# A 448-byte tile ahead of the split weights' buffers in a one-layer transformer kernel

## The chip, the cores and the metric

The kernel runs on one core of one Trainium2 chip. The metric is the time of one execution on the device, in microseconds (us), as the median of several runs; lower is better.

## The reference

One layer over 512 tokens of width 1024, all in float32. What matters here are its matrix products:

```python
xn = rms_norm(h, norm_mix_g)
proj = xn @ w_in                                   # 1024 -> 4008 columns, cut into nine parts
# branch A: 8 heads of causal attention with forget gates; branch B: 8 latent heads with rotary keys
merged = gate_a * (ya @ w_branch_a) + gate_b * (yb @ w_branch_b)
h = h + merged @ w_out                             # 1024 -> 1024
hn = rms_norm(h, norm_ffn_g)
h = h + (silu(hn @ w_gate) * (hn @ w_up)) @ w_down # 1024 -> 2816 -> 1024
y = rms_norm(h, norm_final_g)
```

## The kernel before

Every product is made three times: each float32 operand is split into a part rounded to float32r (`hi`) and the rest (`lo`), and `mm3` (L124) adds hi x hi, hi x lo and lo x hi into one PSUM bank. `split` (L98) makes the parts: ScalarE writes `hi`, VectorE subtracts and writes `lo`. A matrix multiply on the tensor engine has two operands in SBUF: a stationary one of 128 columns, which a weight load (LDWEIGHTS, engine PEld in the profile) brings in, and a moving one of up to 512 columns (MATMUL, engine PE). The profile names a matmul as out<-moving,stationary.

The work goes in stages: the narrow columns of `w_in`; attention, with the remaining projections run between its steps (gates `pg<-x..`, queries and keys `pqa`, values `pva`, latent heads `pqb`, `pkb`, `pvb`, branch outputs `pb`); the output projection `po`; SwiGLU's gate and up strips (`pg<-h..`, `pu`, L932); and the down projection `pd` (L953), whose second column half cuts the last token tile into two parts of 256 columns (L958).

Weights come in pieces of 512 KB. `weights` (L130) takes a raw buffer (tag `wr`), loads it and calls `split_weights`, which takes three rotating buffers each for the parts:

```python
hi = big.tile([P, a, b], F32R, name="whi", tag="pt" if spare else "wh", bufs=4 if spare else 3)
lo = big.tile([P, a, b], F32R, name="wlo", tag="pt" if spare else "wl", bufs=4 if spare else 3)
```

All other large operands lie in the 17 buffers of 8192 bytes of the tag `u8`: `xTh`/`xTl`, `hTh`/`hTl`, `yah`.., `act`, `mgh`/`mgl`, `cq`, `kvs`, and for the output projection alone also the split weights `woh`/`wol` (L892).

The buffers of one partition lie one behind the other in the order in which their tags are first asked for, each rounded up to 32 bytes. From the tag `pt` on they are: 4 x 6656 bytes of `pt`, 1024 of `c1`, 17 x 8192 of `u8`, 2048 of `krs`, 4 x 2048 of `p`, then `rcol` and `post` with 16 bytes each, then 3 x 4096 of `wh` and 3 x 4096 of `wl`. The sizes up to `p` are multiples of 512, so `pt`, `u8`, `krs` and `p` begin at one place modulo 512 bytes; `rcol` and `post` take 32 bytes each, so `wh` and `wl` begin 64 bytes further on. Slices of operands that go into full matmuls begin at multiples of 512 bytes within their buffers. So a pair of operands is at equal places modulo 512 when both are in `pt` or `u8`, and 64 bytes apart when one is in `wh` or `wl`. In the first strip of the up projection, the pieces for the second half of the 1024 inputs go into `pt` (`spare`, L923, L937).

In the code below, the three parts of a product are made in `mm3`, and the loops that call it set the order of the stationary and moving operands.

Of the kernel before, what the change touches and what calls it, by code (L numbers as in the profile page):

```python
# [41 lines left out]
# columns of `cst`  # L42
# [4 lines left out]
def _turn_constants():  # L47
    """1/(2 pi) for angles cut into digits of 2^21, 2^11 and 2: each digit's share of a turn,
    without whole turns, as a part of 13 bits and the rest."""
    out = []  # L50
    for unit in (2.0 ** 21, 2.0 ** 11, 2.0):
        f = _frac_turn(unit)
        a = round(f * 8192.0) / 8192.0
        out.append((unit, a, f - a))
    return out


def _frac_turn(unit):
    from fractions import Fraction
    # pi to 50 digits  # L60
    pi = Fraction(314159265358979323846264338327950288419716939937510, 10 ** 50)
    t = Fraction(int(unit)) / (2 * pi)
    return float(t - round(t))
# [3 lines left out]
def tile_hybrid_fox_mla_block(  # L67
# [30 lines left out]
    def split(hi, lo, src, scale=None):  # L98
        """hi: src rounded to float32r; lo: what is left of it."""
        if scale is None:  # L100
            one = nc.scalar.copy(out=hi, in_=src)  # L101
            two = nc.vector.tensor_tensor(out=lo, in0=src, in1=hi.bitcast(F32), op=ALU.subtract)  # L102
        else:
            one = nc.scalar.activation(out=hi, in_=src, func=AF.Copy, scale=scale)  # L104
            two = nc.vector.scalar_tensor_tensor(out=lo, in0=src, scalar=scale, in1=hi.bitcast(F32),
                                                 op0=ALU.mult, op1=ALU.subtract)
        if pin[1]:
            tc.keep_in_program_order(one)
            tc.keep_in_program_order(two)

    # the tensor engine's work, and the parting of operands, in the order of the program
# [12 lines left out]
    def mm3(o, a, b, start, stop):  # L124
        """o += a^T b for a and b as (hi, lo)."""
        matmul(o, lhsT=a[0], rhs=b[0], start=start, stop=False)
        matmul(o, lhsT=a[0], rhs=b[1], start=False, stop=False)
        matmul(o, lhsT=a[1], rhs=b[0], start=False, stop=stop)

    def weights(src, a, b, spare=False):  # L130
        """A piece [128, a, b] of a weight (a * b <= 1024) as (hi, lo)."""
        raw = big.tile([P, a, b], F32, name="wraw", tag="wr", bufs=2)
        nc.sync.dma_start(out=raw, in_=src)
        return split_weights(raw, spare)
# [8 lines left out]
    def rsqrt(m, n, name, out=None):  # L143
        """v ** -0.5 for m = -4 v [128, n]: q = exp(-ln(4 v) / 2), then the Newton step q (3 - 4 v q^2)."""
        q = small([P, n], name + "_q")
        nc.scalar.activation(out=q, in_=m, func=AF.Ln, scale=-1.0)
        nc.scalar.activation(out=q, in_=q, func=AF.Exp, scale=-0.5)
        t = small([P, n], name + "_t")
        if n == 1:
            nc.vector.scalar_tensor_tensor(out=t, in0=q, scalar=m, in1=q, op0=ALU.mult, op1=ALU.mult)  # L150
        else:
            nc.vector.tensor_tensor(out=t, in0=m, in1=q, op=ALU.mult)
            nc.vector.tensor_tensor(out=t, in0=t, in1=q, op=ALU.mult)
        r = small([P, n], name + "_r") if out is None else out
        nc.vector.scalar_tensor_tensor(out=r, in0=t, scalar=3.0, in1=q, op0=ALU.add, op1=ALU.mult)
        return r

    def mean4(out, ss, width):
        """-4 times the guarded mean of a sum of squares."""
        nc.vector.tensor_scalar(out=out, in0=ss, scalar1=-4.0 / width, scalar2=-4.0 * EPS, op0=ALU.mult, op1=ALU.add)  # L160

    def mean_rsqrt(parts, width, name, out=None):
        """rsqrt of the mean of squares, from sums of squares [128, 1] in the order they come."""
        m = small([P, 1], name + "_m")
        mean4(m, parts[0], width)
        for p_ in parts[1:]:
            nc.vector.scalar_tensor_tensor(out=m, in0=p_, scalar=-4.0 / width, in1=m, op0=ALU.mult, op1=ALU.add)
        return rsqrt(m, 1, name, out)
# [22 lines left out]
    # before it takes its outputs: rotated q of the latent heads by token tile, the q rows of the chunk mask  # L191
# [4 lines left out]
    # rotary keys and the k rows of the chunk mask; from row 104 on: c in three parts  # L196
# [11 lines left out]
    def load_misc(c):  # L208
        if c == 0:
            # the first products wait for it: in two  # L210
            nc.sync.dma_start(out=mraw[0][:, 1, :], in_=w_in[P:2 * P, MISC0:GATE0])
            return
        raw = big.tile([P, 2, MISCW], F32, name="wraw", tag="wr" if c < 2 else "pt", bufs=2 if c < 2 else 4)
        nc.sync.dma_start(out=raw, in_=w_in[c * 256:(c + 1) * 256, MISC0:GATE0].rearrange("(k p) n -> p k n", p=P))
        mraw.append(raw)
# [19 lines left out]
    # products of zeros bring the tensor engine to its full clock  # L235
# [23 lines left out]
    def to_features(rows, hi, lo, t, tag):  # L259
        """Rows [128, 1024] of token tile t into hi/lo pairs [128, 4, 512]."""  # L260
        for c in range(2):
            pt = bank(tag, "ptr")
            for j in range(4):
                transpose128(pt[:, j * P:(j + 1) * P], rows[:, (4 * c + j) * P:(4 * c + j + 1) * P], ident)
            cols = slice(t * P, (t + 1) * P)
            split(hi[c][:, :, cols], lo[c][:, :, cols], pt.rearrange("p (j n) -> p j n", j=4))
# [4 lines left out]
    def rotary_angles():  # L271
        """cos and sin of positions * inv_freq, step by step."""
# [23 lines left out]
        # sin and cos of half the angle by their series, then of the angle itself  # L296
# [22 lines left out]
    rcol = small([P, NT], "rcol", bufs=1)  # L319
    pin[1] = True  # L320
    for st in "f0 k0 f1 t0 k1 f2 t1 f3 t2 m1 t3 f4 t4 m2 t5 f5 f6 t6 f7 m3 t7 w0 w1".split():
# [11 lines left out]
        else:  # L333
            # squares of x, added up over the tiles of features
# [12 lines left out]
    # 1 / rms by token: down the partitions, and along the columns  # L347
# [50 lines left out]
    def project_va(n):  # L398
        """Values of forgetting heads 4n to 4n + 3."""
# [19 lines left out]
    def gates(m):  # L419
        """Gate columns of tile m: 0..7 of the forgetting branch, 8..15 of the latent one."""  # L420
# [10 lines left out]
        # 1 / (1 + e) = exp(-ln(1 + e)); the bound keeps ln in its range  # L431
# [4 lines left out]
    def narrow(t0, n):  # L436
        """Of the narrow columns of n token tiles: norms of q and kv, forget gates, rotary key."""
# [38 lines left out]
    def step():  # L476
        """The gates' share between two steps of the latent heads' preparation."""
        for _ in range(next(stages, 0)):
            next(pre, None)
# [67 lines left out]
    def rotated_to_features():  # L547
        """Rotated q, scaled, as rows in two parts: four heads to a bank."""
# [14 lines left out]
    def project_b(j):  # L563
        """q and k of latent heads 2j and 2j + 1."""
# [26 lines left out]
    def project_a(j):  # L591
        """q and k of forgetting heads 2j and 2j + 1."""
# [23 lines left out]
        if j == 3:  # L616
            # the place of rbc is for outputs from here on
            moved = big.tile([P, S], F32, name="rbc", tag="krs", bufs=1)
            nc.gpsimd.tensor_copy(out=moved, in_=rbc[0])
            rbc[0] = moved  # L620

    def block(p_, i):
        """Of the packed P^T (keys kc, query q at column 384 kc + q), query block i of keys 0..i."""
        a = p_[:, i * P:(i + 1) * P]
        return bass.AP(a.tensor, a.offset, [a.ap[0], [PTS, i + 1], [1, P]])
# [4 lines left out]
    class Item:  # L630
        """Query block i of head h of branch b."""
# [62 lines left out]
    def branch(b, m2, done):  # L694
        """Tiles 2 m2 and 2 m2 + 1 of a branch's projection."""
# [47 lines left out]
    def running_sum():  # L743
        """c, the running sum of the logs of the forget gates, as rows in three parts."""
# [19 lines left out]
        # the first and the last cover all of the columns  # L764
# [15 lines left out]
    class Filler:  # L780
        """Projections to run between the steps of the attention, in order; weights in us of PE."""
# [62 lines left out]
    for n, it in enumerate(items):  # L844
        goal = rest + per * (len(items) - n - 1)
        if n and items[n - 1].i == NT - 1 and items[n - 1].h == NH - 1:
            # the branch's projection may follow at once
# [84 lines left out]
    for s in range(NHC // 2):  # L932
        # the first tiles take the first half of the tokens ahead of the rest
# [18 lines left out]
    ssf = small([P, 2 * NT + 1], "ssf", bufs=1)  # L952
    for half in range(2):  # L953
        nn = slice(half * 512, (half + 1) * 512)
        # parts of the columns, each with a bank: the last tile of the tokens in two
# [94 lines left out]
```

## Time and profile before

| what | value |
|---|---|
| time, median of 3 runs | 756.17 us (756.05 to 757.05) |
| span of the profiled execution, from first to last instruction | 754.7 us |
| PE busy | 739.7 us, 98% of the span |
| weight loads busy | 608.4 us, 81% |
| VectorE, ScalarE busy | 423.2 us, 336.1 us |
| HBM read | 66.59 MB, 91 GB/s over the span |

Of the profiled execution the profile gives the span alone; the median of the runs is 1.5 us above it. A matmul's busy time runs from its start to the modelled end of its pipeline, and two neighbours overlap; how fast matmuls follow each other is read from the distance of their starts in the timeline, not from the length of one.

### The profile page before, as it was taken

The numbers are of one execution on the slowest core, as the hardware profiler recorded it, in microseconds if no ns is written. First come the engines' busy times: TensorE is split into PE (matmuls) and PEld (weight loads), VectorE is DVE, ScalarE is ACT, GpSimd is POOL, SyncE is SP. The second block draws the span as 40 slices with busy tenths as digits, with TensorE's granted clock in tenths as the row PEclk, the third lists the DMA queues.
The fourth block names the chain that finished last, engine by engine and source line by source line (L and its number), as shares of the span: only waits on it lengthen the run. The fifth ranks groups of instructions, "written<-read, shape, count | busy, mean of one in ns | idle before, by whom it ended". The sixth has DMA issues, their size and how long they took to land.

```text
span 754.7 us, 9511 instructions
## 1 busy us (share of the span) xinstructions
PE 739.7 (98%) x3601; PEld 608.4 (81%) x3601; DVE 423.2 (56%) x818; ACT 336.1 (45%) x635; POOL 71.7 (10%) x87
## 2 busy tenths in 40 slices
PE   6999999999999999999999999999999999999996
PEld 4988677879888888887898888888888888888885
DVE  6998987666898986566733332233333233115224
ACT  7457977556675774534423223223232232113213
POOL 4243331011130120200000000000000000000000
PEclk9999999999999999999999999999999999999998
DMA  8522212031232221365303233232333322322312
GB/s 278 169 56 57 57 32 57 30 84 30 85 80 62 69 73 58 109 224 166 90 25 112 83 104 92 85 111 83 89 108 84 99 97 84 112 84 93 103 57 111
DMA packets 68941, 69.45 MB, mean 92 GB/s; under 512 B 3808, under 2 KB 58352, under 8 KB 68896
## 3 DMA queue, kind: packets, MB, share of 16 engines
q1 hardware_dynamic: 66240, 64.91, 28.5%
q10 hardware_dynamic: 1824, 3.38, 1.3%
q0 software_dynamic: 832, 0.57, 0.3%
q8 instruction: 28, 0.46, 0.2%
q14 instruction: 17, 0.14, 0.1%
HBM read 66.59 MB, written 2.10 MB: 91 GB/s over the span
## 4 chain that ended last, share of the span: by engine, by line
PE 90%; DVE 4%; ACT 3%; DMA 2%; issue 1%; SPq 0%; ACTq 0%; DVEq 0%
PE pg L115 26%; PE pu L115 16%; PE pd L115 15%; PE pqa L115 6%; PE pb L115 6%; PE po L115 6%; PE sp L115 4%; PE pva L115 3%; PE py L115 3%; PE pt L120 2%; DMA wraw<-in_w_in_dram 1%; PE pqb L115 1%; DMA wraw<-in_w_kv_up_dram 0%; PE ptr L120 0%; ACT xTh L104 0%
## 5 line engine op out<-in xcount | busy, mean ns | idle before, releaser
L102 DVE TENSOR_TENSOR wlo<-wraw,whi 128x1024 fp32r<-128x1024 f32 x102 | 125.2, 1227 | 205.3 <-ACT whi L101 204.8
L101 ACT CAST whi<-wraw 128x1024 fp32r<-128x1024 f32 x102 | 106.9, 1049 | 217.9 <-PE pu L115 81.6
L115 PE MATMUL pd<-whi,act 128*128 128x512 f32 (+1 forms) x396 | 110.6, 366 | 0.0
L115 PEld LDWEIGHTS pd<-whi,act 128*128 128x128 f32 x396 | 71.2, 188 | 12.4
L115 PE MATMUL pd<-wlo,act 128*128 128x512 f32 (+1 forms) x198 | 72.4, 366 | 0.0
L115 PE MATMUL pg<-hTh,wlo 128*128 128x512 f32 (+1 forms) x192 | 72.4, 377 | 0.0
L115 PE MATMUL pu<-hTh,whi 128*128 128x512 f32 (+1 forms) x192 | 72.3, 377 | 0.0
L115 PE MATMUL pu<-hTl,whi 128*128 128x512 f32 (+1 forms) x192 | 72.3, 377 | 0.0
L115 PE MATMUL pu<-hTh,wlo 128*128 128x512 f32 (+1 forms) x192 | 72.3, 377 | 0.0
L115 PE MATMUL pg<-hTl,whi 128*128 128x512 f32 (+1 forms) x192 | 72.2, 376 | 0.0
L115 PE MATMUL pg<-hTh,whi 128*128 128x512 f32 (+1 forms) x192 | 72.1, 376 | 0.0
L115 PE MATMUL pg<-xTh,whi 128*128 128x512 f32 x128 | 52.9, 413 | 0.0
L115 PE MATMUL pg<-xTl,whi 128*128 128x512 f32 x128 | 50.6, 395 | 0.0
L115 PE MATMUL pg<-xTh,wlo 128*128 128x512 f32 x128 | 50.5, 395 | 0.0
L115 PEld LDWEIGHTS pd<-wlo,act 128*128 128x128 f32 x198 | 37.2, 188 | 6.7
L115 PEld LDWEIGHTS pg<-hTh,whi 128*128 128x128 f32 x192 | 36.2, 188 | 7.3
L115 PEld LDWEIGHTS pu<-hTh,whi 128*128 128x128 f32 x192 | 36.2, 188 | 7.3
L115 PEld LDWEIGHTS pu<-hTl,whi 128*128 128x128 f32 x192 | 36.2, 188 | 7.2
L115 PEld LDWEIGHTS pu<-hTh,wlo 128*128 128x128 f32 x192 | 36.2, 188 | 7.2
L115 PEld LDWEIGHTS pg<-hTh,wlo 128*128 128x128 f32 x192 | 36.1, 188 | 7.2
L115 PEld LDWEIGHTS pg<-hTl,whi 128*128 128x128 f32 x192 | 36.1, 188 | 7.2
L432 POOL TENSOR_SCALAR gate<-gate 128x512 f32<-128x512 f32 x16 | 28.2, 1760 | 118.4 <-ACT gate L430 118.2
(280 smaller groups left out, 1437.0 us busy)
## 6 DMA issues: line engine op xcount, KB each, us to landing
wraw<-in_w_in_dram SPq DMA_DIRECT2D x28, 512.0 KB, 3.9
wraw<-in_w_ffn_gate_dram SPq DMA_DIRECT2D x22, 512.0 KB, 3.7
wraw<-in_w_ffn_up_dram SPq DMA_DIRECT2D x22, 512.0 KB, 3.8
wraw<-in_w_ffn_down_dram SPq DMA_DIRECT2D x22, 512.0 KB, 3.7
wraw<-in_w_out_dram SPq DMA_DIRECT2D x8, 512.0 KB, 4.3
xf<-in_xT_dram SPq DMA_DIRECT2D x8, 256.0 KB, 5.3
wraw<-in_w_branch_b_dram SPq DMA_DIRECT2D x4, 512.0 KB, 3.5
wraw<-in_w_branch_a_dram SPq DMA_DIRECT2D x4, 512.0 KB, 3.4
```

The source lines that it names most:

```text
L101: one = nc.scalar.copy(out=hi, in_=src)
L102: two = nc.vector.tensor_tensor(out=lo, in0=src, in1=hi.bitcast(F32), op=ALU.subtract)
L115: ins = nc.tensor.matmul(*args, **kw)
L120: ins = nc.tensor.transpose(*args)
L432: nc.gpsimd.tensor_scalar(out=g, in0=g, scalar1=1e30, scalar2=None, op0=ALU.min)
```

## The change

A tile of 112 float32 values (448 bytes a partition) is taken from the pool right after `rcol`, ahead of the first request for `post`, `wh` and `wl`, and GpSimd writes zeros into its first two columns. Nothing reads it. With it the buffers of `wh` and `wl` begin 64 + 448 = 512 bytes past the common place, which is the same place modulo 512. Comments and docstrings are taken out as well; they make no instructions.

```diff
     rcol = small([P, NT], "rcol", bufs=1)
+
+    shift = small([P, 112], "shift", bufs=1)
+    nc.gpsimd.memset(shift[:, 0:2], 0.0)
     pin[1] = True
     for st in "f0 k0 f1 t0 k1 f2 t1 f3 t2 m1 t3 f4 t4 m2 t5 f5 f6 t6 f7 m3 t7 w0 w1".split():
```

## Rows read from the trace of the kernel before

**Rows 1.** The page: busy time by engine, and the chain's shares by engine.

```profile
PE 739.7 (98%) x3601; PEld 608.4 (81%) x3601; DVE 423.2 (56%) x818; ACT 336.1 (45%) x635; POOL 71.7 (10%) x87
...
PE 90%; DVE 4%; ACT 3%; DMA 2%; issue 1%; SPq 0%; ACTq 0%; DVEq 0%
```

**Rows 2.** Waits: who waited for whom, us in total, times, longest.

```profile
ACT whi L101 <- PE pu L115: 81.6, 19, 4.6
...
PE pm L115 <- DVE mlo L102: 5.5, 2, 3.4
```

**Rows 3.** Busy time of engines in stretches; PEclk is the granted clock.

```profile
331.00:378.00 47.00, 46.20 (x211) 37.74 (x210) 32.01 (x51) 20.03 (x37) 0.00 (x0) 1.00 0.49 159
...
402.00:627.00 225.00, 225.00 (x971) 181.48 (x970) 74.97 (x81) 61.61 (x80) 0.00 (x0) 1.00 0.32 96
```

**Rows 4.** Timeline of PE (start us, length us), output projection: sixty matmuls apart.

```profile
355.61 0.39 PE L115 MATMUL po<-woh,mgh 128*128 128x512 f32 x1
...
369.21 0.39 PE L115 MATMUL po<-woh,mgh 128*128 128x512 f32 x1
```

**Rows 5.** Timeline of PE, gate and up strips: 195 matmuls apart.

```profile
560.02 0.40 PE L115 MATMUL pg<-hTl,whi 128*128 128x512 f32 x1
...
605.52 0.39 PE L115 MATMUL pg<-hTl,whi 128*128 128x512 f32 x1
```

**Rows 6.** Timeline of PE, down projection, first column half: 108 matmuls apart.

```profile
640.27 0.39 PE L115 MATMUL pd<-wlo,act 128*128 128x512 f32 x1
...
664.99 0.39 PE L115 MATMUL pd<-wlo,act 128*128 128x512 f32 x1
```

**Rows 7.** Timeline of PE, first up strip: 24 matmuls between each two rows.

```profile
385.92 0.28 PE L115 MATMUL pu<-hTh,whi 128*128 128x256 f32 x1
...
388.74 0.28 PE L115 MATMUL pu<-hTh,whi 128*128 128x256 f32 x1
...
391.62 0.28 PE L115 MATMUL pg<-hTh,whi 128*128 128x256 f32 x1
```

**Rows 8.** Timeline of PE, last part of the down projection: 33 matmuls apart.

```profile
743.74 0.28 PE L115 MATMUL pd<-wlo,act 128*128 128x256 f32 x1
...
747.48 0.28 PE L115 MATMUL pd<-wlo,act 128*128 128x256 f32 x1
```

**Rows 9.** Chain that ended last: start us, us, piece, instructions in it.

```profile
63.24 9.11 PE pg L115 x39
...
88.78 1.39 PE pqb L115 x6
...
118.86 1.40 PE pqa L115 x6
...
186.51 2.12 PE pva L115 x18
...
296.99 12.60 PE pg L115 x54
309.59 22.40 PE pb L115 x96
```

**Rows 10.** Groups of instructions by shape: count, busy us, mean ns, idle before.

```profile
L115 PE MATMUL pd<-whi,act 128*128 128x512 f32 x308 | 98.2, 391 | 0.0
L115 PE MATMUL pg<-hTh,whi 128*128 128x512 f32 x160 | 63.3, 396 | 0.0
...
L115 PE MATMUL pva<-whi,xTh 128*128 128x256 f32 x64 | 18.8, 294 | 0.0
...
L115 PE MATMUL pd<-whi,act 128*128 128x256 f32 x88 | 17.8, 276 | 0.0
```

**Rows 11.** Groups on VectorE and GpSimd: count, busy us, mean ns, idle before.

```profile
L102 DVE TENSOR_TENSOR wlo<-wraw,whi 128x1024 fp32r<-128x1024 f32 x102 | 125.2, 1227 | 205.3 <-ACT whi L101 204.8
...
L102 DVE TENSOR_TENSOR wol<-wraw,woh 128x1024 fp32r<-128x1024 f32 x8 | 9.8, 1222 | 7.8 <-ACT woh L101 7.8
...
L612 POOL MEMSET ha<- 6x512 f32 x8 | 4.3, 538 | 0.0
```

## The prediction

> **What bounds the kernel now.** I read the page first, for which engine sets the end: PE is busy for 98% of the span and is 90% of the chain that ended last [rows 1]. The list of waits says the same from the other side: the longest total wait of a PE matmul for another engine is 5.5 us, at the start, while ScalarE waits 81.6 us for PE to give back the up strip's weight buffers [rows 2]. So behind the first 40 us the time is a sum over matmuls, and what counts is how far apart their starts are.
>
> That is not in the mean length of a matmul, so I went to the timeline next and took the step, the distance of starts divided by the matmuls between, for full matmuls (128x512) of the same type in stretches where nothing else bounds:
>
> - output projection: (369.21 - 355.61) / 60 = 226.7 ns [rows 4];
> - gate and up strips: (605.52 - 560.02) / 195 = 233.3 ns [rows 5];
> - down projection: (664.99 - 640.27) / 108 = 228.9 ns [rows 6].
>
> The granted clock is 1.00, the 2.4 GHz level, in the stages of the first two [rows 3], and none of the three runs shows a wait. What differs is where the operands lie. In `po` both are in `u8` buffers, at equal places modulo 512. In the strips the stationary operand is in `wh` or `wl`, 64 bytes further on than the moving one. In `pd` it is the other way round. PE loads the next weights while the present matmul streams (both are busy most of the span, [rows 1]), so the two reads run at the same time, and the step is 6.6 ns longer where the weights lie one way apart, 2.2 ns where the other. The change puts all of these into the case of `po`.
>
> Half-width matmuls (128x256) tell another story, and I did not leave them out. In the first up strip 24 of them with weights in `wh` take (388.74 - 385.92) / 24 = 117.5 ns each, and the 24 behind them, whose weights lie in `pt` at equal places, (391.62 - 388.74) / 24 = 120.0 ns [rows 7]. The last part of `pd`, 64 bytes apart, steps at (747.48 - 743.74) / 33 = 113.3 ns [rows 8]. Equal places are best at 512 columns and worst at 256.
>
> **The change part by part.**
>
> The memset: the nearest row is a GpSimd memset of 538 ns [rows 11]. GpSimd is busy for 10% of the span [rows 1], and behind the new instruction on its queue stand only the additions of squares, which wait for ScalarE anyway. I take nothing; without that cover it is 0.5 us. The tile is written once and read by nobody, so it adds no wait.
>
> The splits: their outputs move by 448 bytes. `wlo` took 1227 ns at the old place and `wol`, already at the new one, 1222 [rows 11]. Nothing.
>
> Gate and up strips, full width: 160 matmuls in each of six groups [rows 10], 960 in all, from 233.3 to 226.7 ns: 960 x 6.6 = 6.4 us less. The floor is 226.7, under which no full matmul steps in any of these rows; the other end is no gain.
>
> Gates, queries and keys, branch outputs (128x512, weights in `wh`): some 750 between 40 and 331 us, but in short runs. Here I had to choose. The latent heads' `pqb`, at equal places already, take 1.39 us for six in such a run, and `pqa`, 64 bytes apart, 1.40 us [rows 9]: a run of six gains 0.01 us only, as if the good step needed a run to settle. The timeline has some 50 runs of six, which give 0.5 us, and some 50 of three, to which I give nothing. Three long runs, 39, 54 and 96 matmuls at 9.11 / 39 = 233.6 and 22.40 / 96 = 233.3 ns [rows 9], are worth 6.6 ns each; the last two follow each other. Leaving out nine at each start for settling (an allowance: a run of six has hardly gained yet), 162 x 6.6 = 1.1 us. Together 1.6 us less; the ends are 0 and, if every one of the 750 gained, 5.0.
>
> `pva`, half width, 64 matmuls in each of three groups [rows 10]: from 2.12 / 18 = 117.8 ns [rows 9] to 120.0, so 192 x 2.2 = 0.4 us more. If they went to 113.3 instead it would be 0.9 less.
>
> The first gate and up strip, half width: 144 matmuls from 117.5 to 120.0 ns, 0.4 us more; the other 48 are in `pt` already. At 113.3: 0.6 less.
>
> Down projection: 308 full matmuls with `whi` and half as many with `wlo`, 462; 88 and 44 half ones [rows 10]. The first column half has 264 full ones: 264 x 2.2 = 0.6 us less. The second alternates nine full with six half ones. By [rows 7] the 132 half ones go from 113.3 to 120.0, 0.9 us more, and the 144 full ones that stand between them have no long run to settle, so I take 1.39 / 6 = 231.7 ns [rows 9] against 228.9: 0.4 more. The last 54 gain 0.1. Sum 0.6 us more; the ends are 1.0 less (all full ones at 226.7, the half ones unchanged) and 1.5 more.
>
> Sum: - 6.4 - 1.6 + 0.4 + 0.4 + 0.6 = - 6.6 us. The profiled execution's span of 754.7 us becomes 748.1; the median of the runs is 1.5 us above the span, and I keep that: 756.2 - 6.6 = 749.6 us. The kernel stays bound by PE: a weight piece in the strips serves 24 matmuls, 24 x 226.7 = 5.4 us, and costs VectorE 1.2 us. With every term at its good end the sum is - 6.4 - 5.0 - 0.9 - 0.6 - 1.0 = - 13.9, 742.3 us; with all but the strips at their bad ends it is - 6.4 + 0.4 + 0.4 + 1.5 + 0.5 = - 3.6, 752.6 us.
>
> **The rivals.**
>
> *It does nothing.* All rows at 226.7 ns have both operands in `u8`, all those at 233.3 have one in `wh` or `wl`, the last large buffers of the partition. If it is the part of the memory that counts, or the product's kind, and not the place modulo 512, then 448 bytes change nothing: 756.2 us. Against it: `pd` and the strips both pair `u8` with `wh`, with the sides exchanged, and differ by 4.4 ns, and `pt` against `wh` differs with the opposite sign [rows 7], which one slow region doesn't give.
>
> The Trainium skill would have it so: "TensorE: Matmul & The Clock Gate", section "Step-by-step: what each phase is for", says that the tensor engine has two independent read ports and that loading the next weights takes no read bandwidth from the running matmul, and "SBUF — State Buffer", section "Who interferes with whom", that PE never waits on another engine. By these an operand's place could not matter, and the sum would be 0. The trace does not agree as it stands: 226.7 against 233.3 ns for the same shape at the same clock [rows 3 to 5].
>
> *The strips never settle.* A run at equal places must get into its good step, and something in the strips, the change of the weight buffer every 24 matmuls or of the PSUM bank every three, throws it out each time. At 231.7 ns the strips give 960 x 1.6 = 1.5 us, the long runs of attention 0.3, the short ones 0.5, against 1.9 lost on half-width matmuls: 755.8 us. Against it: the 60 matmuls of [rows 4] include changes of bank and keep their step.
>
> *Slower.* The equal case at full width is that at half width doubled, 240.0 ns, and `po` owes its step to something else, such as activations as stationary operand. Then the strips cost 960 x 6.7 = 6.4 us more, `pd` 462 x 11.1 + 132 x 6.7 = 6.0, attention 750 x 6.7 = 5.0, `pva` and the first strip 0.8: 18 us, 774 us. It decides against the change from a strip step of 233.3 ns upward. For it speak [rows 7], the very pair of strip weights and `hT` at equal places; against it [rows 4], where the width is the strips' own.
>
> **How the numbers follow.** The forecast has 74%, with a range of its own from 743.5 to 752.6 us; no effect 11%; unsettled strips 6%; slower 9%. The range takes in the forecast and the unsettled strips, 80%: 743.5 to 756.0 us; its low end lets all terms but a small part of the short runs gain. A difference of 0.2% is about what a measurement of this kernel can tell from no change; it is 1.5 us. So faster 74%, the same 17% (no effect and unsettled), slower 9%.
>
> **What would show it.** In the changed kernel's timeline the strips step at 226.7 ns over 96 and more matmuls, and a strip of 96 takes 21.8 us in place of 22.4. The `pb` run of 96 ahead of the output projection falls from 22.40 to some 21.8 us. `po` stays at 226.7. The last part of `pd` goes from 113.3 to 120.0, and `pva` from 117.8 to 120.0: if it doesn't, those terms were wrong by some 1 us each. Strips at 233.3 mean that the place modulo 512 is not the cause; at 240, that half width was the better guide. Other things that would make the prediction wrong: another order of instructions, seen as buffers of `u8` that change places or as new waits of PE, or a softmax chain in attention that PE has to wait for once its own work there is shorter.

## The result and the profile after

The changed kernel takes 749.42 us (median of 4 runs, 748.74 to 750.98) against 756.11 us before on the same chip (755.99 to 757.05): ratio 0.9904, 95% interval 0.9885 to 0.9922. The forecast was 749.6. The profiled execution took 749.56 us with a span of 747.8, 6.9 us shorter than before.

The page after, busy time by engine: only PE's share of the work got shorter, by 9.4 us, and GpSimd has one instruction more.

```profile
PE 730.3 (98%) x3601; PEld 608.4 (81%) x3601; DVE 423.0 (57%) x818; ACT 335.9 (45%) x635; POOL 72.0 (10%) x88
```

The matmuls stand in the same order in both kernels, and all operands but the weights in `wh` and `wl` lie where they lay, so each matmul can be compared with itself. The timeline of PE, with the same pairs as in the rows of before: 195 matmuls of the strips apart, 108 of the down projection, 33 of its last part, 24 of the first up strip.

```profile
549.92 0.39 PE L115 MATMUL pu<-hTh,whi 128*128 128x512 f32 x1
...
594.12 0.39 PE L115 MATMUL pu<-hTh,whi 128*128 128x512 f32 x1
...
633.10 0.39 PE L115 MATMUL pd<-wlo,act 128*128 128x512 f32 x1
...
657.58 0.39 PE L115 MATMUL pd<-wlo,act 128*128 128x512 f32 x1
...
736.65 0.28 PE L115 MATMUL pd<-wlo,act 128*128 128x256 f32 x1
...
740.61 0.28 PE L115 MATMUL pd<-wlo,act 128*128 128x256 f32 x1
...
385.06 0.28 PE L115 MATMUL pu<-hTh,whi 128*128 128x256 f32 x1
...
387.93 0.28 PE L115 MATMUL pu<-hTh,whi 128*128 128x256 f32 x1
```

The strips step at 44.20 / 195 = 226.7 ns (233.3 before, [rows 5]), `pd` at 24.48 / 108 = 226.7 (228.9, [rows 6]), the last part of `pd` at 3.96 / 33 = 120.0 (113.3, [rows 8]), the first up strip at 2.87 / 24 = 119.6 (117.5, [rows 7]). All four steps came within half a nanosecond of what was foretold, two of them for the worse.

Chain that ended last, pieces with start, length and count. They answer to [rows 9]:

```profile
118.86 1.39 PE pqa L115 x6
...
186.62 2.16 PE pva L115 x18
...
296.45 12.27 PE pg L115 x54
308.72 19.05 PE pb L115 x84
```

`pva` steps at 2.16 / 18 = 120.0 ns, `pb` at 19.05 / 84 = 226.8, and a run of six `pqa` gained 0.01 us. The chain leaves PE behind 84 of the 96 `pb`; by their starts in the timeline all 96 take 21.76 us in place of 22.40.

Behind them comes the output projection. PE enters it 1.5 us earlier than before and leaves it only 0.9 us earlier. In both kernels PE waits in it for VectorE to add a finished `po` to the residual (`ha`), which VectorE does behind the splits of the arriving weights. The longest of these waits, in brackets, before, after, and in the kernel with the tile behind `wl` (the first experiment below), where all places are as before:

```profile
349.36 0.50 PE L115 MATMUL po<-woh,mgh 128*128 128x512 f32 x1 [0.81 <-DVE ha L907]
```

```profile
348.42 0.50 PE L115 MATMUL po<-woh,mgh 128*128 128x512 f32 x1 [0.95 <-DVE ha L910]
```

```profile
348.71 0.50 PE L115 MATMUL po<-woh,mgh 128*128 128x512 f32 x1 [0.41 <-DVE ha L910]
```

From the first to the last `po` start it is 46.5 us before and 47.0 after, but 46.0 with the tile behind `wl`, and 46.0 to 47.6 in five other executions whose steps are those of equal places. So the 0.6 us lost there vary from one execution to the next and do not come with the places.

Where the 6.9 us come from, by how much earlier the same matmul starts in the timeline after:

| place | earlier by, us |
|---|---|
| `pq` of the latent heads, at 52.66 us before | -0.5 (later) |
| in attention, at 118 us | 0.0 |
| first `pb` of branch A | 0.87 |
| first `po` | 1.51 |
| last `po` | 0.94 |
| end of the first gate and up strip | 0.65 |
| first `pd` | 7.03 |
| first `pd` of the second column half | 7.63 |
| last `pd` | 6.86 |

The first row, before and then after:

```profile
52.66 0.76 PE L115 MATMUL pq<-upw,cq 128*128 128x256 f32 x5
```

```profile
53.12 0.76 PE L115 MATMUL pq<-upw,cq 128*128 128x256 f32 x5
```

Up to there PE has waits for its inputs, and the executions differ whatever the places: in the profiled ones of the experiments below this `pq` starts from 0.2 us earlier to 1.3 us later than before. From there to the first `po` the gain is 1.51 + 0.46 = 2.0 us. It is 2.0 to 2.1 us in five other executions whose steps are those of equal places, and 0.0 with the tile behind `wl`.

### The profile page after: what moved, and what is told of

It is laid out like the page before. It is cut to its first block, busy times and chain, and to the rows that moved or that the text cites. A ratio compares the mean times of both kernels' runs of the same rounds, so it can differ in the third digit from the quotient of the medians.

```text
span 747.8 us, 9512 instructions
## 1 busy us (share of the span) xinstructions
PE 730.3 (98%) x3601; PEld 608.4 (81%) x3601; DVE 423.0 (57%) x818; ACT 335.9 (45%) x635; POOL 72.0 (10%) x88
## 4 chain that ended last, share of the span: by engine, by line
PE 90%; DVE 4%; ACT 2%; DMA 2%; issue 1%; SPq 0%
PE pg L115 26%; PE pd L115 16%; PE pu L115 16%; PE pqa L115 6%; PE pb L115 6%; PE sp L115 4%; PE po L115 4%; PE pva L115 3%; PE py L115 3%; PE pt L120 2%; PE pm L115 2%; DMA wraw<-in_w_out_dram 1%; DMA wraw<-in_w_in_dram 1%; PE pqb L115 1%; ACT sq L340 1%
```

## The experiments

What they ask: is it the place and nothing else that came with the tile; which place, modulo what, and with which sign; and what do half-width matmuls and short runs do?

**The tile behind `wl`.** Memset and tile stay, the tile is asked for later:

```diff
-    shift = small([P, 112], "shift", bufs=1)
-    nc.gpsimd.memset(shift[:, 0:2], 0.0)
     pin[1] = True
...
     pin[1] = False
+    shift = small([P, 112], "shift", bufs=1)
+    nc.gpsimd.memset(shift[:, 0:2], 0.0)
```

> The 448-byte tile and its memset stay, but the tile is asked for behind wl, so wh and wl lie where they lay before, 64 bytes past the common place. Place theory (the place modulo 512 of wh and wl against u8 is all that matters): strips step at 233.3 ns again, the run of 96 pb takes 22.4 us, the time is that of before, 756.1 +- 1 us. Rival (the added instruction or another order of work made the gain): strips at 226.7 ns and 749.4 us.

756.42 us against 756.76, ratio 0.9996 (0.9986 to 1.0005). The instruction is worth nothing, nor is the tile itself.

**Equal places without the tile.** `rcol` and `post` move into spare columns of other buffers, which takes 64 bytes out from before `wh`:

```diff
-    posr = small([P, NT], "posr", I32, bufs=1)
+    posr2 = small([P, 2 * NT], "posr", I32, bufs=1)
+    posr = posr2[:, 0:NT]
...
-    rcol = small([P, NT], "rcol", bufs=1)
+    rcol = posr2[:, NT:2 * NT].bitcast(F32)
...
-        post = small([P, NT], "post", bufs=1)
+        post = rv(20)[:, HALF:HALF + NT]
```

> No tile and no memset: rcol and post move into spare columns of earlier buffers, so wh and wl move 64 bytes down instead of 448 up and lie at the common place modulo 512. Place theory: strips step at 226.7 ns, the last part of pd at 119 to 120 ns, time 749.4 +- 1 us. Rival (it is the absolute address, or the distance of more than 512 bytes, that counts): anything else, 756.1 us if nothing changes for the strips.

748.78 us, ratio 0.9893 (0.9879 to 0.9908). The gain needs neither the tile nor its 448 bytes.

**64 bytes ahead instead of behind.** `small([P, 112], ...)` becomes `small([P, 96], ...)`.

> The tile has 384 bytes in place of 448: wh and wl now begin 64 bytes ahead of the common place. Place theory with a sign (what counts is how far the stationary operand lies behind the moving one): the strips take over the step that pd had before, 228.9 ns, and pd the step that the strips had, 233.3 ns; half-width pd goes from 113.3 to about 117.5. Strips 960 x 4.4 = 4.2 us less than before, pd 462 x 4.4 + 132 x 4.2 = 2.6 us more, attention about 0.7 less: 756.1 - 2.3 = 753.8 us. Rival (each product has a good and a bad step of its own, whatever the sign): strips at 233.3 or 226.7 and pd at 228.9 or 227.7, so 756 or 749.5 us.

752.6 us, ratio 0.9942 (0.9926 to 0.9959): between the two kernels, 1.2 us under what was expected. The miss lies in attention, which gained 2.2 us from the `pq` at 52.7 us to the first `po`, not 0.7. That is as much as with equal places: the `pb` run of 96 gains less (21.98 us, against 21.76), but `pva` gets faster. Busy time of engines in a stretch of the strips and one of `pd`; the count behind PE's time says how many matmuls fell into it. First the tile behind `wl`, where all lies as before, then 64 bytes ahead, then equal places without the tile:

```profile
550.00:600.00 50.00, 50.00 (x216) 40.26 (x215) 15.86 (x18) 13.53 (x17) 0.00 (x0) 1.00 0.33 95
635.00:660.00 25.00, 25.00 (x111) 20.48 (x110) 4.90 (x4) 4.69 (x5) 0.00 (x0) 1.00 0.35 106
```

```profile
550.00:600.00 50.00, 50.00 (x220) 41.00 (x220) 17.95 (x20) 14.10 (x19) 0.00 (x0) 1.00 0.33 95
635.00:660.00 25.00, 25.00 (x109) 20.14 (x108) 4.90 (x4) 4.25 (x5) 0.00 (x0) 1.00 0.33 106
```

```profile
550.00:600.00 50.00, 50.00 (x222) 41.44 (x221) 18.60 (x22) 14.55 (x19) 0.00 (x0) 1.00 0.33 95
635.00:660.00 25.00, 25.00 (x112) 20.72 (x111) 6.13 (x5) 5.24 (x5) 0.00 (x0) 1.00 0.28 87
```

The strips go up from 216 to 220 matmuls, and `pd` goes down from 111 to 109: by their starts 228.9 and 233.1 ns. The two kinds of product exchanged their steps when the sign was turned. So it is not the kind of product and not the far end of the memory.

**Only the `lo` weights moved.** The tile is asked for between `wh` and `wl`, in `split_weights` (ahead of which `shift = []` stands), and not behind `rcol`:

```diff
         hi = big.tile([P, a, b], F32R, name="whi", tag="pt" if spare else "wh", bufs=4 if spare else 3)
+        if not shift:
+            shift.append(small([P, 112], "shift", bufs=1))
+            nc.gpsimd.memset(shift[0][:, 0:2], 0.0)
         lo = big.tile([P, a, b], F32R, name="wlo", tag="pt" if spare else "wl", bufs=4 if spare else 3)
```

> The tile stands between wh and wl: the lo weights are at the common place, the hi weights 64 bytes past it. Theory that each matmul pays for the weight load that runs beside it: two of three loads bring hi weights and pay 6.6 ns, one doesn't, so strips at (2 x 233.3 + 226.7) / 3 = 231.1 ns, 2.1 us less than before there, 753.5 us in all. Rival (the good step is a state that needs every pair at equal places): strips at 233.3 ns, 756.1 us, or beyond it.

756.31 us, ratio 0.9997 (0.9987 to 1.0006). The time is the rival's, the strips' step is not: 231.1 ns, to the tenth what the adding theory says: 218 matmuls in the stretch of the strips, where the tile behind `wl` had 216. `pd` took it all back, with 109 where that had 111: its full matmuls went up from 228.9 to 232.5 ns, its half ones from 113.3 to 118.9.

```profile
550.00:600.00 50.00, 50.00 (x218) 40.63 (x217) 16.23 (x18) 13.52 (x17) 0.00 (x0) 1.00 0.33 95
635.00:660.00 25.00, 25.00 (x109) 20.16 (x108) 4.90 (x4) 5.03 (x5) 0.00 (x0) 1.00 0.33 106
```

A sum over pairs doesn't explain that, and below it fails altogether.

**Matmuls alone.** A kernel that computes nothing of the reference: 96 matmuls in a row of each kind, between two buffers at equal places modulo 512, with an offset added to the stationary one:

```python
a = d // 4 + 128 * k
nc.tensor.matmul(po[0:w, 0:cols], lhsT=st[:, a:a + w], rhs=mv[:, 512 * k:512 * k + cols], ...)   # k = i % 4
```

> A kernel of matmuls alone, which computes nothing of the reference: 96 in a row of each kind, float32r, the stationary operand a given number of bytes past the moving one modulo 512. Place theory: at 512 columns 226.7 ns at 0, 512 and 1024 bytes, 233.3 at 64 and 576, 228.9 at 448, others between or above; the same value at equal places modulo 512 whatever the full distance. At 256 columns 120.0 at 0, 117.5 at 64, 113.3 at 448. With 32 stationary columns the weight load is four times shorter and the step at 64 bytes falls towards 226.7. Rival (kind of product or buffer, not place): one step for all places, and one for each width.

Groups by shape, count, busy us and mean ns; the names say the place: zero 0, odd 32, pair 64, quad 128, six 192, half 256, ten 320, twelve 384, last 448, turn 512 bytes.

```profile
L186 PE MATMUL wide_pair<-mv,st 128*128 128x512 f32 x96 | 22.6, 395 | 0.0
L186 PE MATMUL wide_ten<-mv,st 128*128 128x512 f32 x96 | 22.6, 395 | 0.0
...
L186 PE MATMUL wide_quad<-mv,st 128*128 128x512 f32 x96 | 22.5, 395 | 0.0
L186 PE MATMUL wide_twelve<-mv,st 128*128 128x512 f32 x96 | 22.5, 395 | 0.0
...
L186 PE MATMUL wide_six<-mv,st 128*128 128x512 f32 x96 | 22.1, 391 | 0.0
L186 PE MATMUL wide_last<-mv,st 128*128 128x512 f32 x96 | 22.1, 391 | 0.0
...
L186 PE MATMUL wide_half<-mv,st 128*128 128x512 f32 x96 | 21.9, 389 | 0.0
L186 PE MATMUL wide_turn<-mv,st 128*128 128x512 f32 x96 | 21.9, 389 | 0.0
L186 PE MATMUL wide_zero<-mv,st 128*128 128x512 f32 x96 | 21.9, 389 | 0.0
L186 PE MATMUL mid_half<-mv,st 128*128 128x256 f32 x96 | 11.7, 283 | 0.0
L186 PE MATMUL mid_zero<-mv,st 128*128 128x256 f32 x96 | 11.7, 283 | 0.0
L186 PE MATMUL mid_pair<-mv,st 128*128 128x256 f32 x96 | 11.5, 281 | 0.0
L186 PE MATMUL mid_last<-mv,st 128*128 128x256 f32 x96 | 11.0, 276 | 0.0
```

The steps, each the mean distance of the last 48 starts of a group:

| stationary behind moving, bytes | 0 | 32 | 64 | 128 | 192 | 256 | 320 | 384 | 448 | 512 | 576 | 1024 |
|---|---|---|---|---|---|---|---|---|---|---|---|---|
| 512 columns, ns | 226.7 | 233.3 | 233.3 | 232.4 | 228.9 | 226.7 | 233.3 | 232.4 | 228.9 | 226.7 | 233.3 | 226.7 |
| 256 columns, ns | 120.0 | | 117.8 | | | 120.0 | | | 113.3 | | | |

The settled steps of the strips, of `po` and of `pd`, before and after, are in this table at their places, with no other engine at work beside PE and a granted clock of 1.00. (`pva` before the change is not: see the end of the next section.) And the table says more than the change claims: at full width the pattern repeats after 256 bytes, not 512. One expectation failed: with 32 stationary columns the step is 231.7 ns at 0 and at 64 bytes alike, not nearer to 226.7.

**Half of 512.** If 256 is the modulus, a tile of 192 bytes (`small([P, 48], ...)`) must do as well. What was expected of it before the table was known:

> The tile has 192 bytes: wh and wl begin 256 bytes past the common place, half of 512. Place theory: strips and pd get the same step, since 256 is as far one way as the other, and it lies between 226.7 and 240 ns; the step is that of the 256-byte row of the table of matmuls alone. Rival (distance of 64 bytes either way is special, all others are good): strips and pd both at 226.7 ns, 749.4 us.

748.9 us in one run, strips and `pd` with 222 and 112 matmuls in the two stretches, as with equal places:

```profile
550.00:600.00 50.00, 50.00 (x222) 41.42 (x221) 18.61 (x21) 14.55 (x19) 0.00 (x0) 1.00 0.33 95
635.00:660.00 25.00, 25.00 (x112) 20.71 (x111) 6.13 (x5) 5.24 (x5) 0.00 (x0) 1.00 0.30 96
```

The time is the rival's, but its reason is not: by the table 32 and 128 bytes are bad places too. What holds is the row of 256 bytes. It was timed again in four runs, of which this was expected:

> The 192-byte tile again, timed. If the place counts modulo 256 and not 512, as its one look and the table of matmuls alone have it, the time is that of the 448-byte tile: 749.4 +- 1 us, ratio 0.990. Rival (512 is the modulus and the one look was luck): 752 us or more.

749.68 us, ratio 0.9912 (0.9896 to 0.9929), the same as with 448 bytes.

**Another common place.** `rcol` and `post` go into the buffer of `gcol`, `small([P, KC + 2 * NT], "gcol", bufs=1)`: `pt` and `u8` move 32 bytes up, `wh` and `wl` 32 down.

> rcol and post move into the buffer of gcol: all large buffers move 32 bytes up and wh and wl 32 down, so all begin at the same place modulo 512 again, but a place that is no multiple of 64 bytes. Theory that only the distance counts: strips at 226.7 ns and 749.4 us. Rival (each operand must also begin at a multiple of 64): a longer step, such as 233 ns, in po as well, which was at 226.7 in both kernels, and no gain or a loss.

749.41 us in one run, the same 222 and 112 matmuls, and `po` stays at 226.7 ns. The distance counts, not where the pair lies.

**Without the cut of the last token tile**, on top of equal places without the tile:

```diff
         parts = [(t, 0, 512) for t in range(NT)]
-        if half == 1:
-            parts[-1:] = [(NT - 1, 0, 256), (NT - 1, 256, 512)]
```

> Equal places without the tile, and the down projection's last token tile isn't cut into two parts of 256 columns any more, so all of pd is 512 columns wide. Theory (half-width matmuls at equal places cost 119 to 120 ns and unsettle the full ones between them): pd has 528 full matmuls at 226.7 ns, 119.7 us, in place of 462 x 227.7 + 132 x 119.0 = 120.9 us, 1.2 us less of PE; behind the last matmul the uncut part takes some 0.5 us longer to evict, square and scale: 748.1 us against 748.8. Rival (the cut hides more of the end than that): the same or up to 1 us more than 748.8.

748.88 us, ratio 0.9899 (0.9884 to 0.9914): no difference from 748.78 that can be told. First and last `pd` in the timeline of PE, with the cut and then without:

```profile
618.67 0.39 PE L115 MATMUL pd<-whi,act 128*128 128x512 f32 x1
...
739.44 0.28 PE L115 MATMUL pd<-whi,act 128*128 128x256 f32 x1
```

```profile
620.49 0.39 PE L115 MATMUL pd<-whi,act 128*128 128x512 f32 x1
...
739.95 0.39 PE L115 MATMUL pd<-whi,act 128*128 128x512 f32 x1
```

PE needs 119.46 us in place of 120.77, 1.3 less where 1.2 was expected. Behind the last start, up to the ends of the spans (746.5 and 747.9 us), come 7.9 us in place of 7.1. The remaining 0.5 us are below what the runs resolve.

**Matmuls alone, second table**: uneven places, mixed widths, shorter weight loads.

> Matmuls alone, nothing of the reference is computed. Theory that a pair has a price of its own which adds up: two of three stationary operands 64 bytes on give 231.1 ns, two of three moving ones 64 bytes on give (2 x 228.9 + 226.7) / 3 = 228.2. Rival (the moving operand's place changing from one matmul to the next costs by itself): the second at about 232.5, as pd had with only the lo weights moved. Nine full and six half ones in turn at equal places: 9 x 226.7 + 6 x 120.0 = 2760 ns per fifteen if they don't disturb each other, some 30 more if they do; at 448 bytes 9 x 228.9 + 6 x 113.3 = 2740. Half width at 192 bytes as at 448: 113.3. Weight loads of 64, 32 and 16 columns: if the step depends on the place only through the load, the four places draw together as the load gets shorter. Places of 8, 16 and 48 bytes: about 233.

Steps as above, over the last 48 or 135 matmuls of a group:

| what | ns |
|---|---|
| two of three stationary operands 64 bytes on | 233.3 |
| two of three moving operands 64 bytes on | 233.3 |
| nine full and six half in turn, equal places, per fifteen | 2780 |
| the same, 448 bytes, per fifteen | 2740 |
| half width at 192 bytes | 117.8 |
| 64 stationary columns, at 0, 64, 128, 192 bytes | 229.9, 232.7, 229.3, 228.4 |
| 32 stationary columns, at 0, 64, 128, 192 bytes | 231.7, 231.7, 230.5, 231.7 |
| 16 stationary columns, at 0, 64, 128, 192 bytes | 231.7, four times |
| 8, 16, 48 bytes | 230.5, 233.3, 233.3 |

The spread over the four places is 6.7 ns with 128 stationary columns (first table), 4.3 with 64, 1.2 with 32, none with 16: the effect of the place goes with the length of the weight load that runs beside the matmul. Prices don't add over pairs: both uneven patterns step at 233.3. Two more expectations failed: half width at 192 bytes steps at 117.8, not 113.3, and 8 bytes at 230.5, not 233. In the mix, a round at equal places costs 2780 - (9 x 226.7 + 6 x 120.0) = 20 ns more than its parts, since the first full ones behind the half ones step at 234, 235, 229, 232, 231 before they settle at 227. At 448 bytes there is no such loss.

## Why the prediction was right

- **PE bounds the kernel, and the step is what to read.** Right. No other engine's work changed, and 6.4 of the 6.9 us lie in the strips.
- **Equal places cause the short step.** Shown. The tile behind `wl` gives nothing; equal places without the tile, at another common place, and half a turn apart all give the whole gain; the turned sign exchanges the steps of strips and `pd`. That rules out the first rival, the part of the memory or the kind of product. The Trainium skill ("TensorE: Matmul & The Clock Gate", section "Step-by-step: what each phase is for") says that loading the next weights takes no read bandwidth from the running matmul. The runs do not agree with it as it stands: for the same shape the first table spans 226.7 to 233.3 ns by the places of the two operands alone.
- **Strips:** 6.4 us foretold, 7.03 - 0.65 = 6.4 measured. The strips settle and stay settled over 960 matmuls, so the rival of unsettled strips falls, and with it the slower one: 226.7 ns, not 240.
- **Attention:** 1.6 less and 0.4 more for `pva`, that is 1.2 net, were foretold; 2.0 were measured, from the `pq` at 52.7 us to the first `po`. The term was mis-sized in several small parts: the three long runs gave 1.2 (1.1 foretold), the runs of six 0.7 (0.5), those of seven to twelve, which the sum leaves out, 0.2, and `pva` cost 0.2. The runs of three gave next to nothing, as foretold.
- **The first strip:** 0.4 more foretold, 0.94 - 0.65 = 0.3 measured.
- **Down projection:** the first column half gained 0.6 as foretold; the second lost 7.63 - 6.86 = 0.8 where 1.2 was foretold. The term that was mis-sized is that of the full matmuls between half ones: they were put at 231.7 ns, the step of a run of six, and stepped at 229.7, since nine in a row are long enough for the last ones to settle. The half ones came to 119.0, not 120.0, because the first of six behind a full one still takes 114.
- **The total is in part luck.** From 52.7 us on and without the output projection, what was measured adds up to 2.0 - 0.3 + 6.4 - 0.2 = 7.9 us less, where 6.6 were foretold. The 0.5 us lost before 52.7 us and 1.51 - 0.94 = 0.6 us lost in the output projection bring it down to 6.9. The sum has neither, and neither goes with the places; equal places without the tile gave 8.0 us by the medians.

Left open: why only `lo` weights at equal places bring the strips to 231.1 ns in the kernel and 233.3 in the table; and the step of half-width matmuls. It is 113.3 at 448 bytes and 117.8 at 192, while `pva` before the change stepped at 117.8 [rows 9] at the very place at which `pd` had 113.3 [rows 8]. With `wh` and `wl` 64 bytes ahead the two are exchanged, in one trace and again at one place: fifteen `pva` take (187.34 - 185.64) / 15 = 113.3 ns each, thirty-three `pd` (743.40 - 739.51) / 33 = 117.9.

```profile
185.64 0.28 PE L115 MATMUL pva<-whi,xTl 128*128 128x256 f32 x1
...
187.34 0.28 PE L115 MATMUL pva<-whi,xTl 128*128 128x256 f32 x1
...
739.51 0.28 PE L115 MATMUL pd<-wlo,act 128*128 128x256 f32 x1
...
743.40 0.28 PE L115 MATMUL pd<-wlo,act 128*128 128x256 f32 x1
```

So at half width the place alone does not set the step at 64 bytes either way. It may depend on how a run was entered; no run here decides it. Nor is the mechanism in the memory shown, only that the effect goes with the length of the weight load.

## What to carry to other kernels

Where PE bounds a kernel, read the distance of starts for each kind of matmul of one shape; if two kinds differ, compare where their stationary and moving operands lie modulo 256 bytes. Small tiles asked for between large buffers set these places; they can go into spare columns, which cost nothing here. Check half-width and short runs on their own: here the place that is best at 512 columns is the worst at 256, and a run of six behind a break has not settled yet. And compare several executions before a difference of half a microsecond is put down to the change: here the start and the output projection varied by that much whatever the places.

## What the runs showed of the hardware

- float32r matmuls of 512 columns step at 226.7 to 233.3 ns by the distance of their operands modulo 256 bytes, at the 2.4 GHz level, without any other engine at work.
- At 256 columns they step at 120.0 ns at equal places; 64 bytes apart, either way, both 113.3 and 117.8 ns occur.
- A shorter weight load is not always better: with one of 16 columns the step is 231.7 ns at all four places tried, longer than the 226.7 with a full one at equal places.
- At equal places, after a break or a change of width, the settled step of 512 columns often comes only after five to ten matmuls: 5 behind half-width ones, 6 in the `pg` run of 54, 10 behind a wait in `po`.
